# Two PSUM banks for projections and five for the scan, with one exponential left in PSUM

## The chip, the cores and the metric

The kernel runs on one core of a Trainium2 chip. The metric is the device time of one execution in microseconds (us). TensorE (PE) multiplies matrices into PSUM, which has eight banks of 128 x 512 fp32; VectorE (DVE), ScalarE (ACT) and GpSimd (POOL) do the elementwise work, and SyncE (SP) issues the DMAs, all in one queue in program order.

## The reference, cut to what matters

One inference step runs 1280 tokens (256 of context, 1024 latent) of width 1024 through two layers. Layer A is attention beside a convolution. Layer C, the one that the change touches, is a bidirectional Mamba-2 scan (`ssd_scan`), in chunks of 128 tokens and for each of 32 heads:

```python
seg = a_cum[:, :, :, None] - a_cum[:, :, None, :]
decay = jnp.exp(jnp.where(causal, seg, -jnp.inf))
cb = jnp.einsum('bclgn,bcsgn->bclsg', cf, bf)
y_diag = jnp.einsum('bclsg,bclsge,bcsgep->bclgep', cb, decay, xdt)
y_off = jnp.einsum('bclgn,bcgepn,bclge->bclgep', cf, prev, jnp.exp(a_cum))
y = (y_diag + y_off).reshape(b, L, G, E, P)
```

It runs once forward and once backward, the two are added, then `y = rmsnorm(y * silu(z)) @ w_out`. Both directions use the same `cb` and `x`, so the kernel adds the two decay matrices before it multiplies: (exp forward + exp backward) x cb.

## The kernel before, in words

Every projection is a product of fp32 values in which both sides are split into a high and a low half; `mm3` (L119 to L121) issues three matmuls for each product. `lin` makes a weight block's outputs in three column groups (256, 512 and 512 tokens). Each group is 24 matmuls into one PSUM bank of the tag "mm" (matrix names `psmm`), and a callback then fetches the bank: `out_a` with a DVE operation (L757), the blocks of x, B and C with an ACT copy to a row `raw` (L840), the gate blocks z with an ACT tanh and a DVE operation (L867, L868), the last product with ACT (`part_c`, L1289) or DVE (L1348). A bank can be written again only when its fetch is done. Weights are split on the way in by ACT (`wh`, L114) and POOL (`wl`, L115).

After the fetch of a block of x, a convolution runs: ACT L845, four DVE operations L848, ACT tanh L851, DVE L852 (this makes the row `cy`). Ten PE transposes (L1036) then bring `cy` to token order through the one bank of the tag "tm" (`pstm`), with ACT copies (L1037) between them, and ACT scales it (L1044).

The scan runs in eight units u of four heads, ten chunks each. Unit u first makes the x blocks of unit u+1 (`in_blocks`), then its own two z blocks, then scans its chunks. In a chunk, `scan_a` makes two exponent matrices on PE (L1136, and the mask L1140) in two banks of the tag "sd" (`pssd`), ACT takes their exponentials into SBUF (L1141, tiles `et`), POOL adds the two (L1148), and DVE multiplies by `cb` (L1149). `scan_b` uses the result on PE (L1166) beside the part from the states (L1161); DVE multiplies that part by the tile `eb` (L1170), which DMA has filled with exp(a_cum) and the skip term (L1123, L1126), sums it (L1175 or L1177), adds (L1178) and gates it (L1179). ACT squares the result back into `eb` (L1181), and POOL sums the squares (L1183, L1184): `eb` is free for its next load only after that. `advance` (L1075 DVE, L1078 PE, L1083 POOL, L1085 DVE) moves a state on by one chunk.

In Python these stages are written one behind the other. The order of an engine's instructions is set when the kernel is built: a scheduler simulates the instructions with their waits and buffers, and interleaves units, projections and scan. A change of buffers therefore changes the order on all engines from the place where the buffers are opened (L736, the first output projection of layer A) to the end.

Of the kernel before, what the change touches and what calls it, by code (L numbers as in the profile page):

```python
# [10 lines left out]
F32 = mybir.dt.float32  # L11
# [3 lines left out]
AF = mybir.ActivationFunctionType  # L15
# [35 lines left out]
def body(nc, tc, d, dbg=None, stop=None):  # L51
    es = ExitStack()
    with es:
        _body(nc, tc, d, es, dbg or {}, stop)


def _body(nc, tc, d, es, dbg, stop):
    V, S, G, PE = nc.vector, nc.scalar, nc.gpsimd, nc.tensor
    dma = nc.sync.dma_start

    def pool(name, bufs=1, space=None, side=None, stack=es):
        kw = {}
        if space is not None:
            kw["space"] = space
        if side is not None:
            kw["side"] = side
        if space is None:
            kw["reuse_waits"] = "tile"
        return stack.enter_context(tc.tile_pool(name=name, bufs=bufs, **kw))
# [9 lines left out]
    def psum_phase(**bufs):  # L79
        st = es.enter_context(ExitStack())  # L80
        p = pool("pp", space=PSUM, stack=st)
        ptags.clear()
        ptags.update({k: (p, n) for k, n in bufs.items()})
        return st
    dp = pool("dp", space=DRAM)

    def psum(tag="x"):
        tag = tag if tag in ptags else "sd"
        p, n = ptags[tag]
        return p.tile([128, 512], F32, name="ps" + tag, tag=tag, bufs=n)  # L90
# [91 lines left out]
    def bcast_cols(r, j0, jn, ps):  # L182
        for j in range(jn):
            PE.matmul(ps[:, j * 128:(j + 1) * 128], r[:, j0 + j:j0 + j + 1].to_broadcast([128, 128]), ident,
                      start=True, stop=True)
        return ps
# [85 lines left out]
    esP = psum_phase(mm=6, x=2)  # L272
# [160 lines left out]
    for c0, n in CHUNKS:  # L433
        ps = psum()
# [63 lines left out]
    esP = psum_phase(s=5, pt=2, po=1)  # L498
# [22 lines left out]
    for c0, n in CHUNKS:  # L521
        ps = bcast_cols(rq, c0 // 128, n // 128, ps=psum("pt"))
# [210 lines left out]
        return  # L733


    esP = psum_phase(mm=3, tm=1, sd=4)  # L736
    x1d = dp.tile([8, 128, T], F32, name="x1d")
    hls.append(pool("hlB1", bufs=16, side="left", stack=esH))
    esR = ExitStack()
# [149 lines left out]
    def dtile(name, dt=F32, tag=None):  # L889
        return dq.tile([128, HT], dt, name=name, tag=tag or name)  # L890
# [40 lines left out]
    p = dtile("p")  # L931
# [43 lines left out]
    for half in range(2):  # L975
        hs = slice(half * 64, half * 64 + 64)
        for c0 in range(0, 5):
            c = half * 5 + c0
            ps = psum("sd")
# [77 lines left out]
    sp = pool("ssd", bufs=2, side="right", stack=esC)  # L1057
# [50 lines left out]
    xas, ebs, cbs, bts = {}, {}, {}, {}  # L1108
# [7 lines left out]
    def load_x(u, c):  # L1116
        xa = xas[c] = sp.tile([128, OXD], F32, name="xa", tag="xa", bufs=3)
        dma(xa, cmb[u, c, :, 0:OXD])
        if u % 2 == 0:
            bts[c] = sp.tile([128, 128], F32, name="bt", tag="bt")  # L1120
            dma(bts[c], cmb[u, c, :, OBT:OBT + 128])
        eb = ebs[c] = sp.tile([128, 2, 3, 128], F32, name="eb", tag="eb")
        dma(eb[:, :, 2], cmb[u, c, :, OXD:OXD + 256].rearrange("p (j t) -> p j t", j=2))  # L1123
        for pr_ in range(2):
            ev = eyd[c, 4 * u:4 * u + 4].rearrange("(j p) d t -> p j (d t)", p=2)[pr_]
            dma(eb[pr_ * 64:pr_ * 64 + 64, :, 0:2].rearrange("p j d t -> p j (d t)"),  # L1126
                ev.unsqueeze(0).to_broadcast([64, 2, 256]))

    def scan_a(u, c):
        xa = xas[c]  # L1130
        ct = xa[:, OCT:OCT + 128]
        mv, lt = mvs[c % NMV], lts[c % NMV]
        pss = [psum("sd") for _ in range(2)]
        es_ = [sp.tile([128, 4, 128], F32, name="et", tag="et", bufs=4) for _ in range(2)]
        for dr, ps in enumerate(pss):
            PE.matmul(ps, lt[:, dr], mv, start=True, stop=False)  # L1136
        for dr, ps in enumerate(pss):
            et = es_[dr].rearrange("p h t -> p (h t)")
            p3, mk = ps.rearrange("p (h t) -> p h t", h=4), maskb[:, dr:dr + 1].to_broadcast([128, 4, 128])
            PE.matmul(p3, identb, mk, start=False, stop=True)  # L1140
            S.activation(et, ps, AF.Exp)  # L1141
        if u % 2 == 0:
            pc_ = psum("sd")
            PE.matmul(pc_[:, :128], bts[c], ct, start=True, stop=True)
            cbs[c] = sp.tile([128, 128], F32, name="cb", tag="cb", bufs=NCH)
            S.copy(cbs[c], pc_[:, :128])
        mt = es_[0]
        G.tensor_add(mt, es_[0], es_[1])  # L1148
        V.tensor_mul(mt, mt, cbs[c].unsqueeze(1).to_broadcast([128, 4, 128]))  # L1149
        return xa, mt  # L1150

# [67 lines left out]
    for u in range(8):  # L1219
# [9 lines left out]
        elif u:  # L1229
            z_block(2 * u)  # L1230
            z_block(2 * u + 1)
        load_x(u, 0)
        load_x(u, 1)
        if u == 7:
            esK.close()
# [4 lines left out]
            for k in range(14):  # L1240
                prep_y(0, k, None, yp[k < 6], "yhl")
        nxt = scan_a(u, 0)
        sf = None
        for c in range(NCH):
            cur, nxt = nxt, (scan_a(u, c + 1) if c + 1 < NCH else None)
            if c + 2 < NCH:
                load_m(u, c + 2)
# [11 lines left out]
            if c + 2 < NCH:  # L1259
                load_x(u, c + 2)  # L1260
# [281 lines left out]
```

## Time and profile before

| what | value |
|---|---|
| runs | 2082.36, 2087.28 (median), 2091.7 us |
| profiled execution | 2085.1 us |
| its span | 2083.3 us, so 1.8 us lie around it |
| granted TensorE clock, mean | 0.987 of full speed |
| busy share PE / DVE / ACT / POOL | 96 / 67 / 42 / 34 % |

The span has five stretches after the attention layer. The output projection of layer A and the start of layer C's projections lie from about 850 to 1100 us. From 1100 to 1748 us projections and scan run interleaved. From 1748 to 1880 us the projections are used up: the end of the seventh unit's scan and the whole eighth unit run there, with the first pieces of the last product (`part_c`) between them. From 1880 us on there is only the last product and the final norm. A PE that is busy for nearly the whole of a stretch can only lose there; where it idles, the wait that ends last decides.

### The profile page before, as it was taken

To read this page: it belongs to the slowest core of one execution; us is meant where nothing else is said; L and a number is where in the kernel's file an instruction comes from. 1 tells how busy PE (TensorE), PEld (TensorE's weight loads), DVE (VectorE), ACT (ScalarE), POOL (GpSimd) and SP (SyncE) were. 2 spreads that over 40 slices of the span, in tenths; PEclk is the share of its full clock that TensorE was granted. 3 is DMA by queue.
4 is the path that set the end of the run, shared out by engine and by line. 5 is a ranking of instruction groups with operands and counts; after the bars stand their busy time and mean duration, and the time that the engine had idled before them with its cause. 6 is when DMAs were issued, how large, how long until landed. Compare 5 with 4: busy or idle time off the path is not lost. (4 is left out here: it accounts for less than half of the span.)

```text
span 2083.3 us, 32430 instructions
## 1 busy us (share of the span) xinstructions
PE 1999.5 (96%) x11830; PEld 1629.6 (78%) x11830; DVE 1391.4 (67%) x2177; ACT 876.8 (42%) x1683; POOL 707.3 (34%) x567
## 2 busy tenths in 40 slices
PE   6999999999999999989999999999999999789997
PEld 4777888777777768868887878887788877579997
DVE  5797897666565763357658586758587666773743
ACT  5411311666565663234644343443344333334531
POOL 1211122213131212543125465545464444552101
PEclk9999999999999999999999999999999999999998
DMA  8424123220222225322567767765776577655442
GB/s 331 170 107 149 53 93 122 75 68 29 62 61 60 67 84 206 124 88 79 163 197 227 223 182 216 227 193 178 214 218 192 178 228 221 210 155 203 133 163 71
DMA packets 273341, 313.57 MB, mean 151 GB/s; under 512 B 21184, under 2 KB 221920, under 8 KB 273184
## 3 DMA queue, kind: packets, MB, share of 16 engines
q1 hardware_dynamic: 273184, 311.51, 47.6%
q8 instruction: 94, 1.54, 0.3%
q14 instruction: 63, 0.52, 0.1%
HBM read 223.38 MB, written 88.05 MB: 149 GB/s over the span
## 5 line engine op out<-in xcount | busy, mean ns | idle before, releaser
L119 PE MATMUL psmm<-hl,wh 128*128 128x512 f32 (+1 forms) x1152 | 424.1, 368 | 4.6 <-ACT wh L114 3.4
L121 PE MATMUL psmm<-hl,wl 128*128 128x512 f32 (+1 forms) x1152 | 422.2, 367 | 4.2 <-POOL wl L115 4.2
L120 PE MATMUL psmm<-hl,wh 128*128 128x512 f32 (+1 forms) x1152 | 423.7, 368 | 0.0
L115 POOL TENSOR_TENSOR wl<-ws,wh 128x1024 fp32r<-128x1024 f32 x89 | 224.5, 2524 | 464.2 <-ACT wh L114 462.1
L121 PEld LDWEIGHTS psmm<-hl,wl 128*128 128x128 f32 x1152 | 218.7, 190 | 36.9 <-POOL wl L115 6.2
L119 PEld LDWEIGHTS psmm<-hl,wh 128*128 128x128 f32 x1152 | 219.0, 190 | 35.9 <-ACT wh L114 4.3
L120 PEld LDWEIGHTS psmm<-hl,wh 128*128 128x128 f32 x1152 | 219.0, 190 | 30.1 <-issue 1.2
L383 DVE SCALAR_TENSOR_TENSOR cacc<-cvin,acw,cacc 128x1295 f32<-128x1295 f32 x120 | 206.9, 1741 | 4.6 <-ACT cacc L378 3.1
L114 ACT CAST wh<-ws 128x1024 fp32r<-128x1024 f32 x109 | 113.5, 1042 | 206.4 <-PE psmm L120 149.2
L848 DVE SCALAR_TENSOR_TENSOR cy<-raw,prm,cy 128x1282 f32<-128x1282 f32 x96 | 162.9, 1697 | 23.6 <-ACT cy L845 15.7
L120 PE MATMUL psmm<-hlo,wh 128*128 128x512 f32 (+3 forms) x480 | 171.4, 358 | 0.0
L119 PE MATMUL psmm<-hh,wh 128*128 128x512 f32 (+3 forms) x480 | 167.7, 359 | 1.7 <-ACT hh L259 1.7
L121 PE MATMUL psmm<-hh,wl 128*128 128x512 f32 (+3 forms) x480 | 169.2, 355 | 0.0
L617 DVE TENSOR_REDUCE mx<-pss 128x1 f32<-128x512 f32 (+1 forms) x208 | 137.3, 668 | 35.3 <-PE pss L121 34.3
L119 PE MATMUL psmm<-yh,wh 128*128 128x256 f32 (+1 forms) x476 | 148.2, 315 | 3.3 <-ACT yh L1205 2.8
L120 PE MATMUL psmm<-yl,wh 128*128 128x256 f32 (+1 forms) x476 | 150.0, 317 | 0.5 <-DVE yl L1206 0.3
L1148 POOL TENSOR_TENSOR et<-et 128x512 f32<-128x512 f32 x80 | 125.1, 1564 | 72.1 <-ACT et L1141 69.7
L121 PE MATMUL psmm<-yh,wl 128*128 128x256 f32 (+1 forms) x476 | 147.8, 314 | 1.4 <-POOL wl L115 1.4
L1083 POOL TENSOR_TENSOR st<-st,dec_bc 128x256 f32<-128x256 f32 x104 | 82.9, 803 | 168.6 <-DVE st L1085 113.4
L626 ACT ACTIVATE prob<-pss,nm 128x512 f32<-128x512 f32 x192 | 130.2, 693 | 16.1 <-DVE nm L621 14.2
L646 PE MATMUL pspt<-ident,prob 128*128 128x128 f32 x800 | 121.7, 278 | 4.7 <-ACT prob L626 3.8
L652 ACT COPY ptile<-pspt 128x512 f32<-128x512 f32 (+1 forms) x144 | 81.2, 568 | 105.3 <-PE pspt L646 104.3
(336 smaller groups left out, 4151.1 us busy)
## 6 DMA issues: line engine op xcount, KB each, us to landing
xa<-cmb SPq DMA_DIRECT2D x80, 384.0 KB
wm<-in_wmod_dram SPq DMA_DIRECT2D x48, 512.0 KB
ws<-in_wc_dram SPq DMA_DIRECT2D x40, 512.0 KB
eb<-eyd SPq DMA_DIRECT2D x160, 128.0 KB
ws<-in_wco_dram SPq DMA_DIRECT2D x32, 512.0 KB
cmb<-xt SPq DMA_DIRECT2D x24, 640.0 KB
bx<-cmb SPq DMA_DIRECT2D x72, 192.0 KB
eb<-cmb SPq DMA_DIRECT2D x80, 128.0 KB
```

Source lines behind the costliest of these rows:

```text
L114: S.copy(wh, ws)
L115: (eng or G).tensor_sub(wl, ws, f32(wh))
L119: PE.matmul(ps, lh, rh, start=start, stop=False)
L120: PE.matmul(ps, lh, rl, start=False, stop=False)
L121: PE.matmul(ps, ll, rh, start=False, stop=stop_)
L383: V.scalar_tensor_tensor(cacc[i], cv[:, k:k + CO], acw[:, 31 * i + k:31 * i + k + 1], cacc[i], ALU.mult, ALU.add)
L617: V.tensor_reduce(mx[:, x:x + 1], ps[:, :n], axis=AX.X, op=ALU.max, negate=len(segs) == 1)
L626: S.activation(prob[:, c:c + n], ps[:, :n], AF.Exp, bias=nm, accum_out=sums[:, x:x + 1])
L646: PE.transpose(ps[:, x * 128:(x + 1) * 128], prob[:, (g + x) * 128:(g + x + 1) * 128], ident)
L848: V.scalar_tensor_tensor(y, raw[:, k:k + RO], ccw[:, 5 * blk + k:5 * blk + k + 1], y, ALU.mult, ALU.add)
L1083: G.tensor_mul(n.rearrange("p (h e) -> p h e", e=64), s.rearrange("p (h e) -> p h e", e=64), dec_ap(u, dr, c))
L1148: G.tensor_add(mt, es_[0], es_[1])
```

## The change

PSUM keeps eight banks, but from the first output projection on "mm" has two of them instead of three, and "sd" five instead of four. In `scan_a` the exponential of the first direction still goes to SBUF (a tile `mt`, three buffers, in place of two tiles with four); that of the second direction is written back in place to its PSUM bank. The addition of the two is done by DVE, which reads that bank, and no longer by POOL. `eb` gets three buffers instead of two.

```diff
-    esP = psum_phase(mm=3, tm=1, sd=4)
+    esP = psum_phase(mm=2, tm=1, sd=5)
...
-        eb = ebs[c] = sp.tile([128, 2, 3, 128], F32, name="eb", tag="eb")
+        eb = ebs[c] = sp.tile([128, 2, 3, 128], F32, name="eb", tag="eb", bufs=3)
...
-        es_ = [sp.tile([128, 4, 128], F32, name="et", tag="et", bufs=4) for _ in range(2)]
+        mt = sp.tile([128, 4, 128], F32, name="et", tag="et", bufs=3)
...
-            et = es_[dr].rearrange("p h t -> p (h t)")
...
-            S.activation(et, ps, AF.Exp)
+            S.activation(ps if dr else mt.rearrange("p h t -> p (h t)"), ps, AF.Exp)
...
-        mt = es_[0]
-        G.tensor_add(mt, es_[0], es_[1])
+        V.tensor_add(mt, mt, pss[1].rearrange("p (h t) -> p h t", h=4))
```

In the changed kernel the new DVE addition is L1146, and lines behind it move up by one or two (L1149 is L1147, L1170 is L1168). PE, ACT and SP have the same instructions as before, in another order; POOL has 80 fewer and DVE 80 more, one for each chunk of each unit.

First, PE at the border between the third and the fourth unit, where the projections of x have ended and those of z begin. `psmm_13112` is the third column group of the first z block before; `pstm` are the transposes of the last x block's row `cy`; `pssd_125..` belong to a chunk of the scan that is under way. Before:

```order
L121 MATMUL psmm_13112<-hl_8550,wl_13054 128x512
L1161 MATMUL pssd_12586<-xa_12516,st_12572 128x128 x2
L1161 MATMUL pssd_12586<-xa_12516,pl_12489 128x128 x2
L1166 MATMUL pssd_12591<-et_12536,xa_12516 64x128 x4
L1036 MATMUL pstm_13031<-ident_63,cy_13021 128x128 x4
L119 MATMUL psmm_13112<-hl_8557,wh_13053 128x512
L120 MATMUL psmm_13112<-hl_8558,wh_13053 128x512
```

In the changed kernel, at the same border, the third column group of the first z block is `psmm_13082`, and the row's transposes are `pstm_13001` and `pstm_13007`:

```order
L1136 MATMUL pssd_13222<-mv1_9077,lt1_9078 128x512
L1136 MATMUL pssd_13223<-mv1_9077,lt1_9078 128x512
L1139 LDWEIGHTS identb_8588
L1139 MATMUL pssd_13222<-maskb_8590,identb_8588 128x512
L1139 LDWEIGHTS identb_8588
L1139 MATMUL pssd_13223<-maskb_8590,identb_8588 128x512
L1036 MATMUL pstm_13001<-ident_63,cy_12991 128x128 x4
L1036 MATMUL pstm_13007<-ident_63,cy_12991 128x128 x4
L119 MATMUL psmm_13082<-hl_8522,wh_13023 128x512
L120 MATMUL psmm_13082<-hl_8523,wh_13023 128x512
```

The third z group started ahead of the transposes, with work of the scan between; now it starts behind both of them, and the two sets of transposes stand directly one behind the other. Fewer matmuls stand between the end of the x block and its transposes.

Second, the SP queue in the scan of the seventh unit. `xa` and `eb` are a chunk's operands; within one kernel a chunk's `eb` has a number four to five above that of its `xa`. Before:

```order
L1118 DMA xa_16834<-cmb_8593 128x768
L1106 DMA pl_16873<-pvd_9085 128x256
L1123 DMA eb_16772<-cmb_8593 128x2x128
L1126 DMA eb_16772<-eyd_8597 64x2x256 x2
L1100 DMA pvd_9085<-st_16848 128x256
L1121 DMA bt_16902<-cmb_8593 128x128
```

In the changed kernel:

```order
L1118 DMA xa_16832<-cmb_8593 128x768
L1114 DMA lt1_9078<-ltd_8596 8x128
L1113 DMA mv1_9077<-mvd_8595 2x512
L1123 DMA eb_16836<-cmb_8593 128x2x128
L1126 DMA eb_16836<-eyd_8597 64x2x256 x2
L1100 DMA pvd_9085<-st_16846 128x256
```

The `eb` behind `xa_16834` was that of the chunk before it; now the load of `eb` stands behind the `xa` of its own chunk, one chunk further ahead of its use.

## Rows read from the trace of the kernel before

**Rows 1.** Page, section 1: busy us, share of the span, instructions.
```profile
PE 1999.5 (96%) x11830; PEld 1629.6 (78%) x11830; DVE 1391.4 (67%) x2177; ACT 876.8 (42%) x1683; POOL 707.3 (34%) x567
```
**Rows 2.** Busy time by stretch: PE, PEld, DVE, ACT, POOL; clock, DMA share, GB/s.
```profile
1100.00:1748.00 648.00, 639.32 (x3749) 521.07 (x3748) 459.23 (x658) 252.13 (x445) 327.89 (x310) 1.00 0.70 206
1748.00:1880.00 132.00, 109.56 (x696) 90.40 (x696) 92.98 (x147) 44.05 (x83) 73.66 (x75) 0.92 0.61 190
1880.00:2083.00 203.00, 190.49 (x1313) 189.81 (x1312) 105.26 (x198) 75.91 (x126) 21.53 (x17) 0.97 0.42 144
```
**Rows 3.** Waits of PE, 1748 to 1880 us: total us, times, longest.
```profile
PE pssd L1078 <- DVE xw L1075: 8.5, 2, 4.4
PE pssd L1136 <- DVE eb L1170: 3.6, 1, 3.6
```
**Rows 4.** Waits of DVE, 1748 to 1880 us.
```profile
DVE eb L1170 <- DMA eb<-eyd: 9.9, 5, 4.4
DVE et L1149 <- POOL et L1148: 6.0, 3, 2.6
```
**Rows 5.** The chain that ended last, 1824 to 1852 us: start, us, what.
```profile
1830.66 3.47 DMA eb<-eyd
1834.13 1.45 POOL et L1148
...
1844.82 7.25 DMA eb<-eyd
```
**Rows 6.** Tile et, whole span: duration in ns min/median/max, first and last start.
```profile
L1141 ACT ACTIVATE et<-pssd x160: 573/596/670, 1095.5 to 1864.6; 128x512 f32<-128x512 f32 x160
L1148 POOL TENSOR_TENSOR et<-et x80: 1262/1294/2557, 1096.7 to 1865.5; 128x512 f32<-128x512 f32 x80
L1149 DVE TENSOR_TENSOR et<-et,cb x80: 672/692/2883, 1102.4 to 1866.9; 128x512 f32<-128x512 f32 x80
...
L1166 PE MATMUL pstm<-et,xa x80: 272/273/324, 1803.6 to 1876.3; 128*64 128x128 f32 x80
```
**Rows 7.** Tile eb, whole span, the DVE product.
```profile
L1170 DVE TENSOR_TENSOR eb<-pssd,eb x80: 410/683/693, 1105.2 to 1877.9; 128x512 f32<-128x512 f32 x64, 128x256 f32<-128x256 f32 x16
```
**Rows 8.** Groups of DVE by shape, 850 to 1900 us: busy, mean ns | idle before.
```profile
L1149 DVE TENSOR_TENSOR et<-et,cb 128x512 f32<-128x512 f32 x80 | 67.1, 839 | 51.3 <-POOL et L1148 47.3 <-ACT cb L1146 4.0
```
**Rows 9.** Timeline of ACT at a border: start, us, instruction.
```profile
1361.02 0.58 ACT L840 COPY raw<-psmm 128x512 f32<-128x512 f32 x1
...
1378.94 1.37 ACT L1044 ACTIVATE ct<-cy,prm 128x1282 f32<-128x1282 f32 x1 [1.73 <-DVE cy L852]
...
1380.98 0.87 ACT L867 ACTIVATE tz<-psmm 128x256 f32<-128x256 f32 x2
```
**Rows 10.** Timeline of DVE at the same border.
```profile
1377.42 1.49 DVE L852 SCALAR_TENSOR_TENSOR cy<-ct,cy 128x1282 f32<-128x1282 f32 x1
```
**Rows 11.** Timeline of PE at the same border.
```profile
1365.79 0.58 PE L119 MATMUL psmm<-hl,wh 128*128 128x512 f32 x1
...
1375.80 0.39 PE L119 MATMUL psmm<-hl,wh 128*128 128x512 f32 x1
1376.48 0.39 PE L119 MATMUL psmm<-hl,wh 128*128 128x512 f32 x1
```
**Rows 12.** Timeline of DVE in the first output projection.
```profile
901.49 0.74 DVE L757 SCALAR_TENSOR_TENSOR xo<-psmm,mcol,xo 128x512 f32<-128x512 f32 x1
...
911.26 0.74 DVE L757 SCALAR_TENSOR_TENSOR xo<-psmm,mcol,xo 128x512 f32<-128x512 f32 x1
```
**Rows 13.** Timeline of PE there; in brackets idle before and what ended it.
```profile
917.54 0.39 PE L119 MATMUL psmm<-hl,wh 128*128 128x256 f32 x1 [3.37 <-ACT wh L114]
```
**Rows 14.** Timeline of SP there.
```profile
902.26 10.09 SPq L759 DMA_DIRECT2D x1d<-xo  x2
```
**Rows 15.** Timeline of PE in the last product.
```profile
1980.99 0.34 PE L119 MATMUL psmm<-yh,wh 128*128 128x384 f32 x1
```
**Rows 16.** Timeline of DVE in the last product.
```profile
1989.91 0.41 DVE L1348 TENSOR_TENSOR ft<-psmm,ryb 128x256 f32<-128x256 f32 x1
```

## Prediction

> **What bounds the kernel now.** The page's first section comes first: PE is busy for 96% of the span [rows 1], so a faster elementwise engine is worth something only where PE still idles. The view of busy time by stretch tells where. Between 1100 and 1748 us PE is busy for 639.3 of 648 us at full clock [rows 2]: only 8.7 us can be won there, while anything that makes PE wait is paid in full. From 1880 us on 12.5 us are idle, nearly all in the last norm, which the change leaves alone. Between 1748 and 1880 us PE idles for 22.4 us of 132, and its granted clock is 0.92, so part of the stretch runs at the lower of its two levels, after stretches in which PE had idled. DVE is busy for 93 us there. The views of waits name what the two engines wait for: PE for DVE's `xw` and for the fetch of a bank by L1170 [rows 3], DVE for the DMA that fills `eb` (9.9 us) and for POOL's addition (6.0 us) [rows 4]. The chain of waits shows the cycle: load of `eb`, POOL addition, DVE's products, then another load of `eb` of 7.25 us on the path [rows 5]. So one late stretch is bound by latency, and all before it by PE, as long as PE finds a free bank.
>
> **The change part by part.** The sum is made against the profiled execution, 2085.1 us (span 2083.3 and 1.8 around it), which is 2.2 us under the median of the runs.
>
> *Addition moved to DVE.* 80 POOL additions of 1.29 us (median; up to 2.56) go [rows 6]. 80 DVE additions come, with one input in PSUM and one in SBUF, 512 columns. The nearest row is L1170, of that form and size: 0.683 us [rows 7]. That is 80 x 0.69 = 55 us on DVE, of which 16 chunks (11 us) stand in the late stretch by the new order, and nearly all the rest before 1748 us. There DVE goes from 459 to about 459 + 64 x 0.69 = 503 us of 648, that is from 71 to 78%. It is hidden beside PE as long as DVE has slack; if that cover were gone it would cost up to 44 us. On the way from exponential to multiplication 1.29 us on POOL turn into 0.69 on DVE, and one crossing between engines goes. The wait of DVE for POOL, 47.3 us over 80 chunks [rows 8], turns into a wait for ACT that ends earlier; behind it on DVE stand state updates and fetches, which it delays less than before. I take 0 for the long stretch, between -8 (all that PE idles there) and +19 (a rival below).
>
> L1149 has a median of 692 ns but a mean of 839 and a maximum of 2883 [rows 6, 8], while L1170 never went over 693 [rows 7]: operations with both inputs in SBUF are stretched at times, the one with an input in PSUM never. The Trainium skill (SBUF — State Buffer, Who interferes with whom) says that a VectorE instruction with two SBUF inputs contends with a GpSimd instruction that reads SBUF, and one with at most one SBUF input does not. The trace agrees; by that rule the new addition keeps its 0.69 us, and with POOL's large addition gone up to 80 x (839 - 692) = 12 us of DVE would come back in L1149 alone. I leave that out of the sum, since DVE has slack where most of it would fall.
>
> *Exponential in place.* ACT writes the same 512 columns (596 ns, rows 6), into PSUM. No row shows that form; the nearest by place are the same line's 573 and 670 ns, so the 80 that move change by at most 80 x 0.07 = 6 us on an engine that is busy for 42%: 0. The bank is now held until DVE's addition, longer than before, and five banks instead of four pay for that: 0.
>
> *Two banks for projections.* With three, a group's bank was wanted again after two other groups had been computed; with two, after one. In the order, the PE work between the end of a group and the next use of its bank falls from a median of 12.8 us to 5.7. A group of 512 columns takes 24 x 0.227 = 5.4 us (three matmuls 0.68 us apart, rows 11). The late fetches stand where the last x block of a unit gives way to z. At the border shown, L840 copies the last group at 1361.02, the convolution ends with L852 at 1377.42 + 1.49, and L1044 and the tanh of the first z groups come behind it on ACT, at 1378.94 and 1380.98 [rows 9, 10]. The first z group had ended by 1365.79, when PE began the next [rows 11]: its fetch came 15 us late. With three banks PE had the second and the third group, the transposes and the scan to do meanwhile. With two it has the second group and the scan, and the new order puts both sets of transposes ahead of the third group; there is one bank for them, and the second set must wait for the copy L1037, queued behind L1044. Walking the new order with the durations of before, I get a stall of 4 to 5.4 us at two of the six borders and 0.5 to 2.6 at the other four, where more of the scan was put in between: 2 x 4.7 + 4 x 1.2 = 14 us. Ends: 4 us (six small ones) and 33 (a whole group, 5.5 us, at each).
>
> In the first output projection DVE fetches groups late, at 901.49 and 911.26 [rows 12]. With two banks the last two groups start up to 7 us later, but PE waits until 917.54 anyway, for weights [rows 13] whose DMA is queued on SP behind a store of 10.09 us from 902.26 [rows 14]. That wait hides the delay: +1 us, 8 if it did not. In the last product a group ended as the next began at 1980.99 and was fetched at 1989.91 [rows 15, 16], 8.9 us later; the new order leaves 5.6 to 8.8 us of work at three such places: +2 us (0 to 5).
>
> *Third buffer of eb, and the late stretch.* An `eb` load had to wait until POOL had summed the squares of the chunk two before; now the load stands behind the `xa` of its own chunk, a chunk earlier, and the POOL addition leaves the cycle [rows 5]. The last unit takes (1876.2 - 1803.6) / 9, about 8.1 us, for a chunk [rows 6]. DVE cannot go below its own work, 93 + 16 x 0.69 = 104 us against 132 now: at most 28 us to win. Of DVE's waits, 15.9 us are those that are loosened [rows 4]. What is late next is `xw`, which waits for `xa`, and the `yl` loads in the same queue. I take half, -14; ends 0 and -28.
>
> The sum: 0 + 14 + 1 + 2 - 14 = +3, so 2088 us against the profiled 2085.1, and 2.2 more for a median: 2090 us.
>
> **The rivals.** *Projections starve on two banks* (slower): at each of the six borders PE stands for a whole third group, because the tanh of the first z group comes over 9 us after its end. That is 33 instead of 14 us: 2109 us. It decides if the tanh stays behind L851 and L1044 on ACT, as at 1380.98 [rows 9]; against it speaks the scan work that the new order puts between. An ACTIVATE that writes to PSUM, says the Trainium skill (ScalarE: Activation LUTs, Step-by-step: what each stage is for), is quicker than one to SBUF, but only useful if TensorE doesn't need most of PSUM. Here PE uses all eight banks; no row of before shows the speed, and the price by that caveat is this rival's.
>
> *The late stretch falls to DVE's work* (faster): `eb` and POOL were all that held it. It takes 104 us, and the borders cost 6: 1 + 6 + 2 - 28 = -19, 2068 us. For it: DVE's own waits there. Against it: the DMA queue, which carries the `xa` and `yl` loads as well.
>
> *The buffer gains nothing*: the load of `eb` is early, but `xa` lands as late as before and takes its place. Then +17: 2104 us.
>
> *DVE becomes the bound of the scan*: the addition delays fetches of the scan's banks by 0.3 us, somewhat under half of its own 0.69, for each of 64 chunks, +19 on top of the forecast: 2109 us. Against it: 22% of idle time on DVE.
>
> **How the numbers follow.** Chances: forecast 0.38, starving 0.25, falling to DVE 0.20, no gain from the buffer 0.12, DVE as bound 0.05. A measurement of this kernel tells about 0.5% (10 us) from no change, so faster means under 2077 and slower over 2098. Faster: 0.18 from the DVE case and 0.06 from the forecast's low end, 0.24. Slower: 0.20 of starving, 0.07 of no gain, 0.03 of DVE as bound and 0.05 of the forecast's high end, 0.35. Same: 0.41. The forecast's own range is 2076 to 2103 (half of its two large terms either way); with the other cases the range is 2066 to 2113.
>
> **What would show it.** PE waits on L119 or L120 for ACT L867 at the borders, 4 to 5 us at two and little at the others (starving: five or more at each); DVE's addition at 0.69 us; the stretch after the last z block shorter by about 14 us, with no wait for `eb` loads left; POOL below 30%; PE busy for 97% or more between those borders. The forecast is wrong if the late stretch hardly shrinks, if PE's waits in the long stretch add up to over 25 us, or if DVE's waits there vanish while PE's grow.

## The result and the profile after

The changed kernel takes 2097.5 us (median of eight runs, 2095.3 to 2105.6) against 2083.5 us for the kernel before on the same chip: 1.0071 times as long, 95% interval 1.0058 to 1.0083, so some 14 us slower. The forecast was a sum of +3 us on the profiled execution of 2085.1, given as 2090 us for a median. The profiled execution of the changed kernel took 2097.4 us (its span is 2095.6), which is +12.3. The sign of the sum and the range held; two of its terms were far off, in opposite directions.

The page's first section, as [rows 1], and the view of busy time by stretch, as [rows 2]:

```profile
PE 2006.5 (96%) x11830; PEld 1633.5 (78%) x11830; DVE 1400.9 (67%) x2257; ACT 883.1 (42%) x1683; POOL 586.5 (28%) x487
```

```profile
1100.00:1748.00 648.00, 629.15 (x3628) 510.13 (x3626) 450.13 (x693) 247.80 (x427) 224.39 (x235) 0.98 0.67 200
1748.00:1880.00 132.00, 117.29 (x766) 96.01 (x767) 103.55 (x188) 52.66 (x98) 56.96 (x70) 0.96 0.72 217
1880.00:2083.00 203.00, 199.38 (x1359) 198.06 (x1359) 107.07 (x188) 76.60 (x126) 19.05 (x14) 0.99 0.39 131
```

In the long stretch PE now idles for 18.9 us (8.7 before), and its granted clock is 0.98 where it was 1.00. Equal times are not equal work any more: the last z block ends at 1776 us instead of 1752. So the loss is better read between marks that both kernels have. The table is worked out from that view in windows of 2 us. It gives PE's idle time, and behind the plus what the lowered clock cost (busy time times one minus the granted clock). Its marks are 850 us, 1100 us, the last z operation on DVE, the last matmul L1166 of the eighth unit (L1164 in the changed kernel), and the end. The last two columns are experiments that follow below.

| stretch | before | changed | changed, banks 3 and 4 | before, banks 2 and 5 |
|---|---|---|---|---|
| 850 to 1100 us | 8.9 + 4.4 | 9.7 + 3.4 | 9.0 + 2.7 | 9.7 + 3.4 |
| to the last z | 8.7 + 0 | 18.8 + 9.3 | 0 + 0 | 40.7 + 8.5 |
| late, to the last L1166 | 22.4 + 8.2 | 14.7 + 3.6 | 13.1 + 6.2 | 23.7 + 9.0 |
| the rest | 12.8 + 0.7 | 14.3 + 3.2 | 13.0 + 0.6 | 17.1 + 4.4 |
| sum | 66.1 | 77.0 | 44.6 | 116.5 |
| span | 2083.3 | 2095.6 | 2060.4 | 2141.7 |

The first two sums differ by 10.9 us, the spans by 12.3: nearly all is accounted for. In the last column it is not: there the sum is 50.4 us above that of the kernel before and the span 58.4, so 8 us stand in time in which the profile counts PE as busy at full clock. The late stretch wins 12.3 us (30.6 to 18.3), the long one loses 19.4 (8.7 to 28.1).

What PE waits for between 1100 and 1748 us (total us, times, longest):

```profile
PE pstm L1036 <- DVE cy L852: 6.1, 5, 2.3
PE pstm L1036 <- ACT xt L1037: 4.3, 3, 1.7
PE psmm L119 <- DVE tz L868: 2.5, 2, 1.4
PE pssd L1078 <- DVE et L1146: 1.8, 2, 0.9
PE pssd L1143 <- DMA eb<-eyd: 1.3, 1, 1.3
```

The first three, 12.9 us, are all at the borders between units: transposes that stand on PE before the convolution has ended, or before ACT has copied the set ahead, and groups that wait for the fetch of z. In order of time the six borders have about 2.7, 1.4, 3.5, 1.0, 3.3 and 1.0 us of them. In the kernel before none of the three was there. At the border of [rows 9 to 11] the timelines of PE, DVE and ACT now show:

```profile
1389.81 0.66 PE L1036 MATMUL pstm<-ident,cy 128*128 128x128 f32 x4 [2.25 <-DVE cy L852]
1391.67 0.91 PE L1036 MATMUL pstm<-ident,cy 128*128 128x128 f32 x4 [1.21 <-ACT xt L1037]
```
```profile
1388.25 1.50 DVE L852 SCALAR_TENSOR_TENSOR cy<-ct,cy 128x1282 f32<-128x1282 f32 x1 [2.07 <-ACT ct L851]
```
```profile
1389.78 1.37 ACT L1044 ACTIVATE ct<-cy,prm 128x1282 f32<-128x1282 f32 x1
1391.06 0.57 ACT L1037 COPY xt<-pstm 128x512 f32<-128x512 f32 x1
1391.52 0.88 ACT L867 ACTIVATE tz<-psmm 128x256 f32<-128x256 f32 x2
```

PE reaches the transposes while L852 has still to run, and the second set waits for a copy that is queued behind L1044. The stretch behind it, and 2 us of it, in the view by stretch:

```profile
1389.00:1398.00 9.00, 6.98 (x26) 5.37 (x27) 4.12 (x7) 3.91 (x7) 0.00 (x0) 0.81 0.37 114
1392.00:1394.00 2.00, 2.00 (x8) 1.36 (x6) 1.11 (x3) 0.98 (x2) 0.00 (x0) 0.50 0.84 258
```

The granted clock is 0.81 over the 9 us and 0.50 in the second row: after the pauses PE runs for a time at 1.2 instead of 2.4 GHz. It does so at four of the six borders (about 1160, 1392, 1615 and 1703 us), and that costs 9.3 us on top of the waits. At the other two (about 1255 and 1478 us) the granted clock stays at 1.00. In the late stretch the waits of DVE for `eb` loads and POOL [rows 4] are gone; these are its largest from 1748 to 1880 us now:

```profile
DVE eb L1168 <- PE pssd L1159: 8.6, 6, 4.2
DVE xw L1075 <- DMA bx<-cmb: 5.5, 4, 2.1
DVE yl L1204 <- ACT yh L1203: 5.2, 4, 2.2
```

PE's own largest waits there end, by the profile, with loads of `mv` and `lt`, the operands of the exponent matrices, where before they ended with DVE [rows 3]:

```profile
PE pssd L1078 <- DMA mv<-mvd: 5.0, 1, 5.0
PE pssd L1136 <- DMA lt<-ltd: 3.2, 2, 1.9
```

The tile of the exponentials, as [rows 6]:

```profile
L1140 ACT ACTIVATE et<-pssd x80: 572/598/608, 1095.4 to 1869.8; 128x512 f32<-128x512 f32 x80
L1146 DVE TENSOR_TENSOR et<-et,pssd x80: 667/676/690, 1098.8 to 1871.1; 128x512 f32<-128x512 f32 x80
L1147 DVE TENSOR_TENSOR et<-et,cb x80: 670/684/1943, 1100.8 to 1871.8; 128x512 f32<-128x512 f32 x80
```

The new addition takes 0.68 us and is never stretched; the multiplication behind it, with both inputs in SBUF, still is. ACT's exponentials by destination, SBUF and PSUM (busy us, mean ns):

```profile
L1140 ACT ACTIVATE et<-pssd 128x512 f32<-128x512 f32 x80 | 47.6, 595 | 103.0 <-PE pssd L1139 102.7
L1140 ACT ACTIVATE pssd<-pssd 128x512 f32<-128x512 f32 x80 | 47.1, 588 | 12.3 <-PE pssd L1139 11.2 <-DVE yz L1173 0.5 <-ACT tz L867 0.2
```

### The profile page after: what moved, and what is told of

The parts are those of the page before. It is cut to its first block, busy times and chain, and to the rows that moved or that the text cites. A ratio compares the mean times of both kernels' runs of the same rounds, so it can differ in the third digit from the quotient of the medians.

```text
span 2095.6 us, 32449 instructions
## 1 busy us (share of the span) xinstructions
PE 2006.5 (96%) x11830; PEld 1633.5 (78%) x11830; DVE 1400.9 (67%) x2257; ACT 883.1 (42%) x1683; POOL 586.5 (28%) x487
## 4 chain that ended last, share of the span: by engine, by line
PE 82%; DVE 7%; DMA 5%; ACT 2%; issue 2%; SPq 1%; POOL 1%; DVEq 0%; ACTq 0%; POOLq 0%
PE psmm L119 17%; PE psmm L120 16%; PE psmm L121 16%; PE pspo L666 5%; PE pspt L646 4%; PE pssd L1078 3%; PE pss L119 3%; PE pssd L1159 2%; PE pss L121 2%; PE pss L120 2%; PE pssd L1164 2%; PE pssd L1136 1%; PE pssd L1139 1%; PE psx L229 1%; PE pstm L1036 1%
## 5 line engine op out<-in xcount | busy, mean ns | idle before, releaser
L119 PE MATMUL psmm<-hl,wh 128*128 128x512 f32 (+1 forms) x1152 | 423.0, 367 | 12.1 <-DVE xo L757 6.3
L119 PEld LDWEIGHTS psmm<-hl,wh 128*128 128x128 f32 x1152 | 220.2, 191 | 47.0 <-issue 5.3
L848 DVE SCALAR_TENSOR_TENSOR cy<-raw,prm,cy 128x1282 f32<-128x1282 f32 x96 | 156.9, 1635 | 20.9 <-ACT cy L845 18.0
L119 PE MATMUL psmm<-hh,wh 128*128 128x512 f32 (+3 forms) x480 | 167.6, 359 | 1.8 <-ACT hh L259 1.8
L119 PE MATMUL psmm<-yh,wh 128*128 128x256 f32 (+1 forms) x476 | 148.8, 316 | 1.9 <-DVE ft L1346 1.8
L646 PEld LDWEIGHTS pspt<-ident,prob 128*128 128x128 f32 x800 | 92.1, 141 | 40.6 <-ACT prob L626 10.5
```

The source lines that it names most:

```text
L119: PE.matmul(ps, lh, rh, start=start, stop=False)
L646: PE.transpose(ps[:, x * 128:(x + 1) * 128], prob[:, (g + x) * 128:(g + x + 1) * 128], ident)
L848: V.scalar_tensor_tensor(y, raw[:, k:k + RO], ccw[:, 5 * blk + k:5 * blk + k + 1], y, ALU.mult, ALU.add)
```

## The experiments

Each kernel was timed against the kernel before on the same chip, in five rounds; a ratio is to that, with its 95% interval. The experiments ran on three chips, on which the kernel before has medians of 2084.1 to 2086.3 us, so kernels of different groups are best compared by their ratios.

**The banks back to three and four.**

```diff
-    esP = psum_phase(mm=2, tm=1, sd=5)
+    esP = psum_phase(mm=3, tm=1, sd=4)
```

> The changed kernel with three banks for projections and four for the scan as before; the exponential in place, DVE's addition and the third buffer of eb stay. Theory A (the two banks cost about 20 to 27 us at the borders between units, their lowered clock included, and buffer and addition give 13 back in the late stretch): about 2070 us, 13 under the kernel before, no PE wait for transposes at the borders. Rival B (the moved addition, or the PSUM bank held until DVE has added, costs the time): near the changed kernel, 2095. Rival C (any new order moves the time by 10 us either way, no part has a size of its own): anything from 2075 to 2095.

Measured: 2062.3 us, 0.9890 (0.9876 to 0.9903). Theory A has the sign, and the gain is larger than it said. To the last z PE does not idle at all:

```profile
1100.00:1742.00 642.00, 642.00 (x3790) 525.51 (x3789) 480.49 (x728) 258.94 (x450) 226.19 (x249) 1.00 0.72 212
```

DVE is busy for 75% there, at full pace for PE. Rivals B and C fall: the addition isn't the cost, and no time this low lay in C's range. With everything else of the change in place, the two banks cost 35.2 us by the spans (2095.6 and 2060.4), 38 by the two ratios. Of the 35.2 the table shows 28.1 before the last z.

**The banks alone.**

```diff
-    esP = psum_phase(mm=3, tm=1, sd=4)
+    esP = psum_phase(mm=2, tm=1, sd=5)
```

> The kernel before with nothing but the banks changed to two and five. Theory A: 2083 + 20 to 27, that is 2103 to 2110 us, slower than the changed kernel, with the late stretch as long as before. Rival B: as before, 2083 us. Rival C: 2075 to 2095, with no relation to the other three.

Measured: 2142.0 us, 1.0268 (1.0252 to 1.0283), more than any theory gave. PE's largest waits between 1100 us and the last z:

```profile
PE pstm L1036 <- DVE cy L852: 12.4, 4, 5.4
PE pssd L1136 <- DVE eb L1170: 3.8, 3, 1.6
PE pssd L1144 <- DMA xa<-cmb: 3.8, 4, 1.5
PE pssd L1161 <- DVE st L1085: 3.2, 1, 3.2
PE psmm L119 <- DVE tz L868: 3.2, 5, 0.8
```

Beside the borders, the scan's own waits come out. That PE has nothing to put over them once the projections stand, with POOL's addition and two `eb` buffers, is my reading of the list and not shown by itself.

**Two buffers of eb.** The changed kernel without `bufs=3` on `eb`:

```diff
-        eb = ebs[c] = sp.tile([128, 2, 3, 128], F32, name="eb", tag="eb", bufs=3)
+        eb = ebs[c] = sp.tile([128, 2, 3, 128], F32, name="eb", tag="eb")
```

> The changed kernel with two buffers of eb as before. Theory A: the gain of the late stretch was mostly the buffer's, so 2097 + 6 to 13, that is 2103 to 2110 us. If POOL's addition was what held the late stretch, not the buffer: 2097, as the changed kernel. Rival B: 2097 or more. Rival C: 2085 to 2105.

Measured: 2125.0 us, 1.0182 (1.0168 to 1.0196): the third buffer is worth 27 us here by the medians and 23 by the ratios, about twice the upper end of theory A. By the account of the table this kernel loses 40.7 us up to the last z (28.1 with the third buffer) and 27.2 in the late stretch (18.3). Against the banks alone it has the addition on DVE and the exponential in place, and is quicker by 18 us by the ratios. DVE's idle time until `eb` loads, over the span (us, times), first in this kernel, then in the changed one:

```profile
  DMA eb<-eyd: 34.8, 16
```
```profile
  DMA eb<-eyd: 7.0, 3
```

**The addition alone.** Both edits above together: three and four banks, two buffers of `eb`, so that of the change only the exponential in place and DVE's addition are left.

> The kernel before with the exponential in place and the addition on DVE alone; banks three and four, two buffers of eb. Theory A: DVE has slack, so between 2075 (if POOL's addition held the late stretch) and 2083 us (if it was the buffer). Rival B: 2090 us or more, since the addition is what costs. Rival C: 2073 to 2093.

Measured: 2063.8 us, 0.9897 (0.9883 to 0.9910). This is below all that was expected, and within 0.1% of the first experiment: with three projection banks the third buffer gives nothing. PE idles for 0.1 us between 1100 us and the last z (8.7 before), and the late stretch loses 15.0 + 5.9 us instead of 22.4 + 8.2. With three banks, all of the gain comes from the addition with the exponential in place.

**The addition on DVE, both exponentials in SBUF.** The kernel before with one letter changed:

```diff
-        G.tensor_add(mt, es_[0], es_[1])
+        V.tensor_add(mt, es_[0], es_[1])
```

> The kernel before with POOL's addition moved to DVE and nothing else: both exponentials stay in SBUF, banks three and four, two buffers of eb. Theory 1 (the addition gains because it leaves POOL, whose operation takes 1.3 us and holds up DVE): about 2064 us, as with the exponential in place. Theory 2 (it gains because one input is in PSUM, so that DVE is not stretched by POOL): 2072 us or more, and the addition itself shows a mean well above 0.69 us.

Measured: 2077.9 us, 0.9959 (0.9945 to 0.9974), 14 us more than with the exponential in PSUM (13 by the ratios): theory 2 for that part. DVE's addition by duration, first here, then in the kernel with the addition alone:

```profile
L1148 DVE TENSOR_TENSOR et<-et x80: 675/692/2120, 1101.0 to 1862.1; 128x512 f32<-128x512 f32 x80
```
```profile
L1146 DVE TENSOR_TENSOR et<-et,pssd x80: 670/680/696, 1098.7 to 1850.5; 128x512 f32<-128x512 f32 x80
```

The medians agree, but with both inputs in SBUF it is stretched up to 2.1 us; in the view of groups by shape its mean is 0.851 against 0.681 us, 13.6 us over 80. By the starts and ends in the trace, all 24 additions that took over 0.75 us here ran beside an instruction of POOL; with one input in PSUM 46 of the 80 did so too, and none of those took over 0.69 us. That the stretching is the whole of the 14 us isn't shown, since the order of the instructions differs as well. By the account of the table this kernel loses 3.3 us up to the last z and 28.8 in the late stretch, against 0.1 and 20.9, while under 4 us of the additions' stretching fall in the late stretch.

**The fifth scan bank, and a second transpose bank.** The changed kernel with two, one and four banks (one bank unused), and with two, two and four:

```diff
-    esP = psum_phase(mm=2, tm=1, sd=5)
+    esP = psum_phase(mm=2, tm=1, sd=4)
```
```diff
-    esP = psum_phase(mm=2, tm=1, sd=5)
+    esP = psum_phase(mm=2, tm=2, sd=4)
```

> The changed kernel with two banks for projections and four for the scan; the eighth bank is not used. Theory 1 (the missing projection bank is the whole cost and the fifth scan bank gives nothing): 2097 us, as the changed kernel. Theory 2 (the fifth scan bank gives part of it back): 2105 us or more.

> The changed kernel with the eighth bank as a second bank for transposes: two, two, four. Theory 1 (the stalls at the borders come from the one transpose bank, whose second set waits for ACT's copy): the waits of transposes for that copy, 4.3 us in all, and their lowered clock go, 2085 to 2090 us. Theory 2 (they come from having only two projection banks, so that PE reaches the transposes before the convolution has ended): the waits for L852 stay and the time is 2095 to 2105 us.

Measured: 2092.0 us, 1.0032 (1.0019 to 1.0045), and 2095.5 us, 1.0050 (1.0038 to 1.0063). The fifth scan bank gives nothing back; without it the kernel is even 0.4% quicker, and no run shows why (the order differs too). Against the first experiment the kernel with two, one and four lacks nothing but the third projection bank, and it is some 30 us slower (ratios 1.0032 and 0.9890): that bank is most of what the split costs.

With two transpose banks PE waits for no transpose at all in the long stretch, and the time doesn't fall. Neither theory fits as a whole: the time is that of theory 2, but the waits for L852 are gone. PE's largest waits from 1100 to 1748 us now stand in the scan and at the fetch of z:

```profile
PE pssd L1136 <- DVE st L1085: 2.8, 5, 1.1
PE pssd L1159 <- POOL st L1083: 2.3, 3, 0.8
PE pssd L1136 <- ACT et L1140: 2.1, 3, 0.7
PE psmm L119 <- DVE tz L868: 1.9, 2, 1.0
```

By the account of the table this kernel loses 12.6 + 1.6 us up to the last z, and the one with two, one and four 13.7 + 1.6, against 18.8 + 9.3 in the changed kernel. So with the fifth scan bank gone the loss there is about half, with a second transpose bank or without. Over the four stretches the sums are 69.0 and 67.9 us against 77.0, but the spans (2096.7 and 2092.0) hardly follow: against the changed kernel some 9 and 6 us more stand in time in which the profile counts PE as busy at full clock, and what they are isn't shown. Half of the stalls before the last z can thus go without the time coming back; how the missing projection bank costs its 30 us beyond these stalls stays open.

**Four projection banks.**

```diff
-    esP = psum_phase(mm=2, tm=1, sd=5)
+    esP = psum_phase(mm=4, tm=1, sd=3)
```

> The changed kernel with four banks for projections and three for the scan. Theory 1 (three projection banks already hide every fetch, as PE did not idle at all between 1100 us and the last z block with three): no gain over 2062 us in the long stretch, and the late stretch, which is scan alone, loses with three banks: 2065 to 2080 us. Theory 2 (projection banks go on paying): 2050 to 2060 us.

Measured: 2098.6 us, 1.0062 (1.0050 to 1.0075): theory 1 in its direction, with a loss far above its range. Projections run ahead (the last z is done at 1694.6 us), and 205 us of scan alone are left, in which PE idles for 37 us and loses 11 to the clock. The fourth projection bank and the missing scan bank aren't separated here.

**The store of z off the SP queue.** In the changed kernel SP waits 40.1 us in all for z rows before it can issue their store (L872, 1100 to 1740 us), against 5.5 us before, and the scan's loads are queued behind it. The rows, first of the changed kernel, then of the one before:

```profile
SPq L872 <- DVE tz L868: 40.1, 8, 11.3
```
```profile
SPq L872 <- DVE tz L868: 5.5, 2, 3.1
```

ACT issues the store instead:

```diff
-        dma(cmb[blk // 2, :, :, OSZ + (blk % 2) * Q:OSZ + (blk % 2) * Q + Q].rearrange("c p t -> p c t"),
+        S.dma_start(cmb[blk // 2, :, :, OSZ + (blk % 2) * Q:OSZ + (blk % 2) * Q + Q].rearrange("c p t -> p c t"),
```

> The changed kernel (banks two and five, three buffers of eb) with the store of the z rows issued by ACT instead of SP. Theory 1 (with two banks the z rows are late, their store waits 40 us in SP's queue in all, and the scan's loads behind it come late): SP's wait goes, PE's waits in the long stretch shrink, 2080 to 2092 us. Theory 2 (PE loses at the borders itself, in the transposes and the fetch of the projection banks, and SP's wait is only a trace of it): 2097 us, as the changed kernel, or more, since ACT now waits for DVE before its next fetch.

> The same with two buffers of eb, so that the scan's loads have less lead. Theory 1: it gains the most here, 2125 minus 15 to 25, that is 2100 to 2110 us, and DVE's waits for eb loads (34.8 us over the span) go down by half. Theory 2: 2120 to 2130 us, the waits for eb loads as before.

> Three banks for projections and four for the scan, exponential in place, DVE's addition, three buffers of eb, and the z rows stored by ACT. Both theories: no gain, since SP waits for z rows only 2.4 us there: 2058 to 2068 us. Any larger move would be the new order of the instructions by itself.

Measured: 2099.0 us, 1.0075 (1.0062 to 1.0088); 2118.4 us, 1.0171 (1.0157 to 1.0186); 2059.9 us, 0.9885 (0.9873 to 0.9898). Theory 1 falls: SP's wait for z is gone from the trace and nothing is won; DVE's idle time for `eb` loads with two buffers is 38.2 us, not half of 34.8. SP's long wait was a sign of late z rows and not a cause. In each of the three pairs the edit changed the order of the instructions and moved the ratio by 0.0011 at most, which speaks against rival C of the first experiments. The last of the three has the lowest median of all, but lies within the interval of the first experiment.

## Why the prediction's range held, and which steps were wrong

*Two banks for projections.* The place was right: the borders, the transposes too early, the second set behind L1037. The walk along the new order gave 14 us of waits, and the waits there are 12.9. They are spread otherwise: about 3 us at three borders and 1.0 to 1.4 at the other three, not 4 to 5.4 at two. The step that failed is the price: it counted the waits alone. After them PE ran at the lower clock, another 9.3 us, although rows of before showed the same behind its idle times in the late stretch. And the scan's own waits, some 6 us, came out in the same stretch. Against three banks, all else equal, the cost is 35 us and not the 17 of the three terms for the banks. The table finds 32 of the 35 us. The two kernels with two projection and four scan banks show that this account isn't the whole mechanism, though: they have half of the loss before the last z, one of them with no wait at a transpose, and still take 30 to 33 us more than with three projection banks. My sign for it was also wrong in its place: I looked for L119 waiting for ACT's tanh; only 2.5 us stand at L119 (they end with DVE's part of the fetch), the rest at the transposes.

*Addition moved to DVE.* Its size (0.68 us) was right, and that DVE has room (75% with three banks, where PE never idles). "I take 0 for the long stretch" failed. Alone, with the exponential in place, the addition removes nearly all of PE's 8.7 us there, the very end that I had bounded it by, and some 9.7 us of the late stretch; the kernel is 22 us faster by the ratio. More than half of this, 13 to 14 us, came only with the exponential in PSUM. The rule of the Trainium skill that I had set beside the sum (SBUF — State Buffer, Who interferes with whom) agrees with these traces: 2120 ns at most with two SBUF inputs on VectorE, 696 with one. I left it out "since DVE has slack"; but DVE's operations lie on the way to PE's next matmul, whatever its busy share. The kernel before shows it in the long stretch, where 8.4 of the 8.7 us that PE idles end with an operation of DVE; the two largest:

```profile
PE pssd L1136 <- DVE eb L1170: 4.1, 4, 1.6
PE pssd L1136 <- DVE st L1085: 3.0, 4, 0.9
```

*Third buffer of eb, and the late stretch.* -14 was close (-12.3), but it was booked to the buffer and bounded to that stretch, and both depend on the banks. With three projection banks the addition alone takes 9.7 us off the late stretch, and the buffer 1.6 more. With two banks the late stretch loses 32.7 us with neither, 27.2 with the addition and 18.3 with both: there the buffer has the larger share, and it is worth 23 to 27 us over the whole kernel. The waits suggest why: DVE waits for `eb` loads with two buffers in both cases (16.5 us with three banks, 34.8 with two), but only with two banks does PE run out of projections to put over them. No experiment shows this by itself.

*Exponential in place.* 588 ns on average against 595 to SBUF: 0, as taken. That five scan banks pay for the longer hold of the bank wasn't needed: with four PE never idles before the last z.

*First output projection and last product.* The two late groups start where it was said, at 902.86 and 912.65 us, each behind L757 (3.6 and 2.4 us idle); up to 1100 us the loss is 13.1 us as against 13.3, so the wait for weights did hide them. The rest from the last L1166 on costs 4.0 us more (forecast +2), 2.5 of it by the clock.

*The rivals.* Projections did starve, but for a transpose or a fetch and not for a whole group. The late stretch did not fall to DVE's work: it still loses 18.3 us. That the buffer gains nothing holds with three banks and not with two. DVE as the bound is excluded by the first experiment, in which it did the same work and PE never idled before the last z.

The two wrong terms had opposite signs: 18 us of cost and some 9 us of gain too little, when the banks are taken as the last step. They cancelled in part, so that +12 was measured where +3 was forecast. That the sum came within 9 us is luck; the range, 2066 to 2113 us, was wide enough for either error alone.

## What to carry to other kernels

An edit with several parts is worth taking apart before it is kept or dropped: here the addition in PSUM wins 22 us and the new split of the banks loses 35. The parts don't add up in any order, though: put into the kernel before by itself, the split loses 56 us, and the third buffer, worth nothing with three projection banks, wins 23 with two. Banks of the engine that bounds the kernel aren't slack to be given away because their median use looks generous: price the places where fetches come late, and beside each pause a lowered clock behind it, which here came at four places of six. And an engine with a quarter of its time free can still be on the path; ask which of its operations the bounding engine waits for.

## What was not expected of the hardware

Behind the waits at the borders, 12.9 us in all, another 9.3 us were lost by the granted clock, although each pause was only 0.4 to 2.3 us long, two or three of them close together at three borders. An addition on DVE of 512 columns took 0.67 to 0.70 us at every one of 80 executions with one input in PSUM, and up to 2.1 us with both in SBUF, and each that took over 0.75 us ran beside an instruction of POOL. ACT's exponential took 588 ns on average into PSUM and 595 into SBUF.
